# Out-projection of a hybrid decoder trunk: six DeltaNet heads by seven products of 2x2 blocks, in the middle of the stage

## The chip, the core and the metric

The kernel runs on one core of one Trainium2 chip. The metric is the device time of one execution in microseconds. Before the change it is 1019.95 us, the median of three runs (1019.5 to 1020.04).

A core has five engines with queues of their own, which run in parallel and wait for each other through semaphores: TensorE (PE, matrix products; PEld is its weight load), VectorE (DVE), ScalarE (ACT), GpSimd (POOL) and SyncE (SP, which here only issues DMAs). Each queue is worked off in order. SBUF is the working memory of 128 partitions, PSUM the memory in eight banks into which TensorE writes.

## What is computed

One decoder layer over 512 tokens and 16 meta tokens, with a model width of 2048. A normalised input goes through one input projection; three mixers run on disjoint heads: gated DeltaNet (6 heads of 128), GLA linear attention (5 heads) and forgetting attention (5 heads, "fox"). Their gated outputs, 6 x 128 + 5 x 128 + 5 x 128 = 2048 columns, go through one output projection, the input is added, and a final RMSNorm follows. Cut to the end, which is what the change touches:

```python
    o_dn = gated_head_norm(o_dn, dz, dn_norm_w.astype(f32))
...
    o_gla = gated_head_norm(o_gla, gz, gla_norm_w.astype(f32))
...
    o_fox = o_fox.reshape(fz.shape) * jax.nn.silu(fz)

    o = jnp.concatenate([o_dn, o_gla, o_fox], axis=-1)[:, PAD:].astype(x.dtype)
    return x + o @ w_out
...
    return rms_norm(h, final_norm_w)[:, N_META:]
```

All inputs and the output are float32.

## The kernel before

**Precision.** The two big projections run as products of split operands: each float32 operand is split into hi (a rounded copy in fp32r, made by ScalarE) and lo (the rest, a subtraction on VectorE). A product is three matmuls: hi by hi, hi by lo, lo by hi (the helper `mms`, line 992; the splits of weights are lines 149 and 150, with a high priority for the planner).

**The planner.** The code is written with a framework that gives each instruction a priority by its place in the program, plays the program on a timeline with assumed durations, and writes down for each engine a fixed order. An instruction of a later part can stand ahead where an earlier one isn't ready on that timeline. Buffers are taken from pools in the same way: a tile waits until one of its pool's buffers is free. So the matmuls of the next projection fill TensorE while a head's attention, a chain of small steps, goes on.

**Pools that matter here.** `wp`: raw, hi and lo buffers of 128x1024 for weights, two of each. `hp`: 32 buffers of 128x528, which hold the split input until the end of the input projection and then the split heads (`part`). `zp`: 11 buffers of 128x512 with the gated outputs of the DeltaNet and GLA heads (`zs`), later the accumulators `acc`. `six`: eight buffers of 128 x 1584, used by the mixers (a fox head takes four: q and k, the gate logits, the hi and the lo part of the probabilities) and by the last five accumulators. `psb` and `psm`: four PSUM banks each.

**Fox heads** (`fox_head`, lines 861 to 940). For each of five heads the projections fk, fv, fq, fz run (`inproj`, line 198; eight of its 128x1024 weight loads per head); then four blocks of 128 queries: scores (lines 903, 904), a softmax on VectorE and ScalarE (907 to 917), transposes (920), hi and lo (923, 924), and one product with the values (936 to 939) which is multiplied into the gate (940). For heads 2 to 4 the gate lies in the tile of the logits.

**The output projection** (from line 976). The 16 heads are the 16 blocks of the sum (six `dz`, five `gz`, five `fz`). `split_o` splits a head into `oh` and `ol` (984, 985). `acc[tb, cc]` is one of 4 x 4 blocks of the output (128 tokens x 512 columns); it is loaded with x by a DMA of ScalarE's queue (1036). For each of the four column blocks `cc`, `run` loads the weights of two heads (128 x 1024: two heads of 512 columns; DMA on SP's queue, line 141) and issues 2 x 4 x 3 matmuls into four banks. `add` (1009) adds a bank to `acc`, `square` (1016) sums its squares on ScalarE, `weigh` (1019) multiplies by the weight of the final norm on POOL. Column block 0 takes 14 heads first and the last two after column block 1. In the last column block the last six heads are done token block by token block from weights split ahead (`load_last`), and each token block is normalised and stored while the next one runs (1077 to 1088). In all, 16 heads x 4 x 4 x 3 = 768 matmuls, six of them (the end of the last token block) in two halves.

Of the kernel before, what the change touches and what calls it, by code (L numbers as in the profile page):

```python
# [8 lines left out]
F32 = mybir.dt.float32  # L9
F32R = mybir.dt.float32r  # L10
# [20 lines left out]
LOW = -87.0  # L31

DN_HEADS, GLA_HEADS, FOX_HEADS = 6, 5, 5
R0 = 32
R1 = R0 + 17

# [38 lines left out]


@with_exitstack
def tile_hybrid_trunk(ctx, tc, xT, xtok, mtok, w_gate, w_in, w_out, consts, lmask, fin_w, out, dbg=None):
# [17 lines left out]
    def t15(name, shape=(P, H, P), dt=F32):  # L96
        return wk.tile(list(shape), dt, tag="t15", bufs=6, name=name)
# [301 lines left out]
    def conv_silu(key, blk, dst, meta=True):  # L399

        t0 = 0 if meta else NM
        pb = row(f"pb{blk}")
        if meta:
            G.memset(pb[:, 0:3], 0.0)
        evac(inproj(key, first=0 if meta else NM - 4), pb, off=3)
        c = row(f"cv{blk}")[:, t0:T]
        V.tensor_scalar_mul(c, pb[:, t0:T], cwc[:, blk, 0:1])
        for w in range(1, 4):
            V.scalar_tensor_tensor(out=c, in0=pb[:, t0 + w : w + T], scalar=cwc[:, blk, w : w + 1], in1=c,  # L409
                                   op0=ALU.mult, op1=ALU.add)  # L410
        silu(dst[:, t0:], c, f"c{blk}")

    def bsl(b):
        return slice(NM + b * P, NM + (b + 1) * P)
# [446 lines left out]
    def fox_head(h):  # L861
# [78 lines left out]
        V.tensor_tensor(out=z, in0=po[:, :512], in1=z, op=ALU.mult)  # L940


    PM = (308, 319)
    for g in range(2):
        for h in range(max(NF, H * g), H * g + H):
# [25 lines left out]
    for mm, n in later:  # L971
# [2 lines left out]
            mybir.DependencyClass.NoSync, mybir.DependencyReason.DATA), reason="behind")  # L974


    heads = [("dz", h) for h in range(DN_HEADS)] + [("gz", h) for h in range(GLA_HEADS)] \
        + [("fz", h) for h in range(FOX_HEADS)]
    oparts = []

    def split_o(i):
        z = zs[heads[i]]
        hi, lo = part(f"oh{i}"), part(f"ol{i}")
        A.copy(hi, z)
        V.tensor_tensor(out=lo, in0=z, in1=hi.bitcast(F32), op=ALU.subtract)
        oparts.append((hi, lo))

    def mms(p_, hi, lo, i, tb, first, last, **kw):
        s = slice(tb * P, (tb + 1) * P)
        oh, ol = oparts[i]  # L990
        for n, (o_, w_) in enumerate(((oh, hi), (oh, lo), (ol, hi))):
            PE.matmul(p_, o_[:, s], w_, start=(first and n == 0), stop=(last and n == 2), **kw)  # L992

    FIRST, LAST = 14, 10
    halves = lambda w: [[t[:, j * 512 : (j + 1) * 512] for t in w] for j in range(2)]
    acc, wl = {}, {}

    def load_last(kp):
        raw = wp.tile([P, 1024], F32, tag="raw", name=f"rawl{kp}")
        nc.sync.dma_start(out=raw, in_=w_out[3, kp])  # L1000
        wl[kp] = []
        for j in range(2):
            hi, lo = part(f"wlh{kp}{j}"), part(f"wll{kp}{j}")
            split(raw[:, j * 512 : (j + 1) * 512], hi, lo)
            wl[kp].append((hi, lo))

    def add(tb, cc, p_, c=slice(0, 512)):
        a = acc[tb, cc][:, c]
# [12 lines left out]
    def run(pa, cc, kp, first, last):  # L1021
        w = halves(load_half(w_out[cc, kp], f"o{cc}_{kp}"))
        for j in range(2):
            for tb in range(4):
                mms(pa[tb], *w[j], 2 * kp + j, tb, first and j == 0, last and j == 1)

    for i in range(FIRST):
        split_o(i)
    fw = []
    for cc in range(4):  # L1030
        for tb in range(4):
            if 4 * cc + tb < 11:
                acc[tb, cc] = zp.tile([P, S], F32, tag="zs", name=f"acc{cc}{tb}")
            else:
                acc[tb, cc] = six.tile([P, S], F32, tag="six", name=f"acc{cc}{tb}")
            nc.scalar.dma_start(out=acc[tb, cc], in_=xtok[tb * P : (tb + 1) * P, cc * 512 : (cc + 1) * 512])
        pa = [psb.tile([P, 512], F32, tag="b", name=f"pa{cc}{tb}") for tb in range(4)]
        n = (FIRST // 2, KT // 2, KT // 2, LAST // 2)[cc]
        for kp in range(n):
            run(pa, cc, kp, kp == 0, kp == n - 1)  # L1040
            if cc == 3 and kp >= 2:
                load_last(kp + 3)
        if cc == 3:
            break
        for tb in range(4):
            add(tb, cc, pa[tb])
            if cc > 0:
                square(tb, cc)
        if cc == 0:
            for i in range(FIRST, KT):  # L1050
                split_o(i)
        if cc == 1:
            pb = [psm.tile([P, 512], F32, tag="m", name=f"pb{tb}") for tb in range(4)]
            run(pb, 0, FIRST // 2, True, True)
            for tb in range(4):
                add(tb, 0, pb[tb])
                square(tb, 0)
    for c in range(4):
        f = part(f"fw{c}").bitcast(F32)
        nc.scalar.dma_start(out=f, in_=fin_w[c * 512 : (c + 1) * 512].partition_broadcast(P))  # L1060
        fw.append(f)
    for cc in range(3):
        for tb in range(4):
            weigh(tb, cc)
    add(3, 3, pa[3], slice(256, 512))
    for tb in range(4):
        cuts = 2 if tb == 3 else 1
        for n in range(cuts):
            c = slice(512 // cuts * n, 512 // cuts * (n + 1))
            p_ = psm.tile([P, 512], F32, tag="m", name="pz") if n else pa[tb]  # L1070
            for i in range(LAST, KT):
                hi, lo = wl[i // 2][i % 2]
                mms(p_[:, c], hi[:, c], lo[:, c], i, tb, n == 1 and i == LAST, i == KT - 1, skip_group_check=True)
            add(tb, 3, p_, c)
            square(tb, 3, c, n)
        r = rr[:, tb : tb + 1]
        V.reduce_sum(r, ss[:, tb, : 3 + cuts], axis=mybir.AxisListType.X)
        A.activation(r, r, AF.Ln, scale=1.0 / D, bias=eps_c)
        A.activation(r, r, AF.Exp, scale=-0.5)
        for cc in (0, 1, 2, 3):  # L1080
            a = acc[tb, cc]
            if cc % 2 == 0:
                A.activation(a, a, AF.Copy, scale=r)
            elif cc == 3:
                V.scalar_tensor_tensor(out=a, in0=a, scalar=r, in1=fw[cc], op0=ALU.mult, op1=ALU.mult)
            else:
                V.tensor_scalar_mul(a, a, r)
            nc.sync.dma_start(out=out[tb * P : (tb + 1) * P, cc * 512 : (cc + 1) * 512], in_=a)


def _layout(x, meta_tokens, norm_w, w_in, conv_w, a_log, dt_bias, dn_norm_w, w_gk2, b_gk,
# [11 lines left out]
    wo = w_out[0].reshape(KT // 2, 2, P, 4, 512)  # L1103
    z6, z5 = np.zeros(6, f), np.zeros(5, f)
    one6, one5 = np.ones(6, f), np.ones(5, f)
    misc = np.zeros((P, 8), f)
# [21 lines left out]
        "w_out": c(wo.transpose(3, 0, 2, 1, 4).reshape(4, KT // 2, P, 1024)),  # L1128
        "consts": c(consts), "lmask": c(lm), "fin_w": c(np.asarray(final_norm_w)),
    }  # L1130

# [14 lines left out]
```

## Time and profile before

| | |
|---|---|
| median of the runs | 1019.95 us |
| the profiled execution | 1018.81 us |
| its span, first to last instruction | 1017.1 us |
| mean granted TensorE clock | 0.998 |
| first and last start of a matmul of the output projection | 825.7 and 1008.9 us |
| end of the last fox head's attention | 870 us |
| DMA traffic | 105 MB, 103 GB/s on average |

The profile is of one execution. "Busy" is the time in which an engine worked on instructions; matmuls are pipelined and overlap, so TensorE's busy time says that it was fed, not how fast it went. An arrow `out<-in` names the tile written and the tiles read; `L992` is line 992 of the kernel. "Idle before" is what an engine did not work just ahead of an instruction, with the instruction that ended the wait.

### The profile page before, as it was taken

To read this page: it belongs to the slowest core of one execution; us is meant where nothing else is said; L and a number is where in the kernel's file an instruction comes from. 1 tells how busy PE (TensorE), PEld (TensorE's weight loads), DVE (VectorE), ACT (ScalarE), POOL (GpSimd) and SP (SyncE) were. 2 spreads that over 40 slices of the span, in tenths; PEclk is the share of its full clock that TensorE was granted. 3 is DMA by queue.
4 is the path that set the end of the run, shared out by engine and by line. 5 is a ranking of instruction groups with operands and counts; after the bars stand their busy time and mean duration, and the time that the engine had idled before them with its cause. 6 is when DMAs were issued, how large, how long until landed. Compare 5 with 4: busy or idle time off the path is not lost.

```text
span 1017.1 us, 18766 instructions
## 1 busy us (share of the span) xinstructions
PE 1006.3 (99%) x7662; PEld 907.4 (89%) x7662; DVE 558.2 (55%) x1226; ACT 416.5 (41%) x916; POOL 135.5 (13%) x141
## 2 busy tenths in 40 slices
PE   9999999999999999999999999999999999999996
PEld 8899999899999888998999979898989888888885
DVE  6376867856566984343838373544444474323333
ACT  7653533443456333344544434333333362223224
POOL 0021411211112221100110021010101000000014
PEclk9999999999999999999999999999999999999999
DMA  9623133233221333222122222322223263232244
GB/s 356 221 68 131 65 99 105 83 100 104 91 79 64 98 104 100 71 79 70 63 65 69 67 92 63 94 92 70 92 82 92 85 204 128 83 104 90 96 145 166
DMA packets 42410, 105.03 MB, mean 103 GB/s; under 512 B 10733, under 2 KB 13981, under 8 KB 42324
## 3 DMA queue, kind: packets, MB, share of 16 engines
q1 hardware_dynamic: 28064, 92.23, 27.3%
q10 hardware_dynamic: 14260, 11.61, 4.1%
q8 instruction: 60, 0.98, 0.4%
q14 instruction: 26, 0.21, 0.1%
HBM read 98.64 MB, written 5.05 MB: 102 GB/s over the span
## 4 chain that ended last, share of the span: by engine, by line
PE 92%; DVE 3%; ACT 2%; DMA 1%; POOL 1%; issue 1%; ACTq 1%; DVEq 0%; POOLq 0%
PE pp L198 57%; PE pa L992 16%; PE pp L252 4%; PE pss L773 1%; POOL stgz L325 1%; PE pgate L352 1%; PE pfo L936 1%; PE pfa L903 1%; DVE ot L507 1%; DVE wlo L150 1%; PE pg L474 1%; PE pa L615 1%; PE py L639 1%; DMA sc<-ab 1%; PE pb L992 1%
## 5 line engine op out<-in xcount | busy, mean ns | idle before, releaser
L198 PE MATMUL pp<-xl,whi 128*128 128x264 f32 (+2 forms) x1456 | 378.6, 310 | 0.0
L198 PE MATMUL pp<-xh,whi 128*128 128x264 f32 (+2 forms) x1456 | 376.1, 310 | 0.1
L198 PE MATMUL pp<-xh,wlo 128*128 128x264 f32 (+2 forms) x1456 | 375.2, 309 | 0.4 <-DVE wlo L150 0.4
L198 PEld LDWEIGHTS pp<-xl,whi 128*128 128x128 f32 x1456 | 244.4, 189 | 13.6 <-issue 0.2
L198 PEld LDWEIGHTS pp<-xh,wlo 128*128 128x128 f32 x1456 | 243.6, 188 | 14.2 <-DVE wlo L150 0.9
L198 PEld LDWEIGHTS pp<-xh,whi 128*128 128x128 f32 x1456 | 243.0, 188 | 14.5 <-issue 0.8
L149 ACT CAST whi<-raw 128x1024 fp32r<-128x1024 f32 x110 | 115.4, 1049 | 201.5 <-PE pp L198 159.8
L150 DVE TENSOR_TENSOR wlo<-raw,whi 128x1024 fp32r<-128x1024 f32 x110 | 134.6, 1224 | 108.5 <-ACT whi L149 98.2
L992 PE MATMUL pa<-whio,ol 128*128 128x512 f32 x224 | 88.1, 393 | 0.0
L992 PE MATMUL pa<-wloo,oh 128*128 128x512 f32 x224 | 88.0, 393 | 0.0
L150 DVE TENSOR_TENSOR wloo<-rawo,whio 128x1024 fp32r<-128x1024 f32 x29 | 35.9, 1236 | 81.2 <-ACT whio L149 81.2
L992 PE MATMUL pa<-whio,oh 128*128 128x512 f32 x224 | 78.0, 396 | 0.0
L149 ACT CAST whio<-rawo 128x1024 fp32r<-128x1024 f32 x29 | 30.4, 1050 | 83.7 <-PE pa L992 65.1
L992 PEld LDWEIGHTS pa<-whio,ol 128*128 128x128 f32 x224 | 42.1, 188 | 9.8
L992 PEld LDWEIGHTS pa<-wloo,oh 128*128 128x128 f32 x224 | 42.1, 188 | 9.4
L992 PEld LDWEIGHTS pa<-whio,oh 128*128 128x128 f32 x224 | 41.9, 188 | 9.2
L325 POOL TENSOR_SCALAR stc<-cv 128x528 f32<-128x528 f32 (+1 forms) x18 | 28.2, 1564 | 138.3 <-DVE cv L409 115.3
L409 DVE SCALAR_TENSOR_TENSOR cv<-pb,cpk,cv 128x528 f32<-128x528 f32 (+1 forms) x54 | 40.8, 755 | 0.7
L1019 POOL TENSOR_TENSOR acc<-acc,fw 128x512 f32<-128x512 f32 x12 | 15.7, 1349 | 159.1 <-DMA fw<-in_fin_w 159.1
L316 DVE TENSOR_TENSOR pb<-pp,rstd 128x264 f32<-128x264 f32 (+1 forms) x36 | 13.7, 422 | 23.3 <-PE pp L198 23.3
L507 DVE TENSOR_TENSOR ot<-ab 51x30 f32<-51x30 f32 (+14 forms) x60 | 21.2, 354 | 3.6 <-DMA ab<-scmeta 2.1
L325 POOL TENSOR_SCALAR stfz<-zfz 128x512 f32<-128x512 f32 x5 | 9.8, 1965 | 99.0 <-ACT whi L149 49.0
(391 smaller groups left out, 1285.4 us busy)
## 6 DMA issues: line engine op xcount, KB each, us to landing
raw<-in_w_in SPq DMA_DIRECT2D x110, 512.0 KB, 3.3
rawo<-in_w_out SPq DMA_DIRECT2D x29, 512.0 KB, 3.3
xt<-in_xtok SPq DMA_DIRECT2D x8, 512.0 KB, 9.8
acc<-in_xtok ACTq DMA_DIRECT2D x16, 256.0 KB, 5.1
out<-acc SPq DMA_DIRECT2D x16, 256.0 KB, 3.0
xs<-in_xT SPq DMA_DIRECT2D x7, 528.0 KB, 6.7
gb<-gd ACTq DMA_DIRECT2D x2, 792.0 KB, 6.1
eg<-gd ACTq DMA_DIRECT2D x8, 192.0 KB, 3.4
```

What stands on the lines that cost most here:

```text
L149: A.copy(hi, raw)
L150: V.tensor_tensor(out=lo, in0=raw, in1=hi.bitcast(F32), op=ALU.subtract)
L198: mm = PE.matmul(p_[:, :nt], wt[:, j * m : (j + 1) * m], xx[k][:, t0 : t0 + nt], start=(k == 0 and wt is hi and xx is xh), stop=(k == KT - ...
L252: mm = PE.matmul(ps[:, :S], wt[:, j * P : (j + 1) * P], xx[k][:, NM:T], start=(k == 0 and wt is hi and xx is xh), stop=(k == KT - 1 and wt ...
L316: V.tensor_tensor(out=o, in0=p_[rows], in1=rstd[rows, t0 : t0 + n], op=ALU.mult)
L325: G.tensor_scalar_max(t, src, LOW)
L352: PE.matmul(pgate[a][:, :HT], wg[k // 8][:, k % 8, :], xx[k][:, a * HT : (a + 1) * HT], start=(k == 0 and xx is xh), stop=(k == KT - 1 and ...
L409: V.scalar_tensor_tensor(out=c, in0=pb[:, t0 + w : w + T], scalar=cwc[:, blk, w : w + 1], in1=c, op0=ALU.mult, op1=ALU.add)
L474: PE.matmul(pg[:r, j * r : (j + 1) * r], kT[:, j, ts], kT[:, j, ts], start=True, stop=True)
L507: V.tensor_tensor(out=t3, in0=a3[:, j + 1 :, j : j + 1].to_broadcast([NN * 4 + H, m, j]), in1=a3[:, j : j + 1, 0:j].to_broadcast([NN * 4 + ...
L992: PE.matmul(p_, o_[:, s], w_, start=(first and n == 0), stop=(last and n == 2), **kw)
L1019: G.tensor_tensor(out=acc[tb, cc], in0=acc[tb, cc], in1=fw[cc], op=ALU.mult)
```

## The change

The rows of the output projection's weights that belong to the DeltaNet heads (768) are taken out of the plain loops and multiplied by a scheme of seven products instead of eight, on blocks of 2 x 2. The left operand is cut by tokens (first and second 256) and by heads (even and odd of a pair, three pairs): a11, a12 (first tokens, even and odd head), a21, a22. The right one is cut by heads and by columns (first and second 1024). With sums of blocks on both sides,

- on the left: s1 = a21 + a22, s2 = s1 - a11, s3 = a11 - a21, s4 = a12 - s2 (on VectorE, in place, `sums`, `differences`), each split into hi and lo by `operand`;
- on the right (x, y, z in `weight_sums`): three differences and one more are computed from w_dn and kept in DRAM (`tw`);
- seven products (`product`): 3 pairs x 4 banks x 3 matmuls each, four of them going on in banks that hold an earlier product; after each, `take` adds four banks to four `acc` blocks.

The weight sums don't depend on the activations. They are made in `fox_head` of heads 0 to 3 in six pieces (pair and column half), each in one tile of `six`: four loads of 256 KB, four subtractions of 128 x 512, four stores of 256 KB, the DMAs on SP's queue.

The order of the stage becomes: the first eight of the ten other heads for column blocks 0 and 1, with the making of the operands between the loads; the seven products; the last two heads for column blocks 0 and 1; ten heads for column block 2; four heads for column block 3; and the end as before. Every third load of a product has its raw, hi and lo buffers in `six` (`load_s`). The first five `acc` blocks lie in `zp`, the others three to a tile of `six`. The loads of the final norm's weight stand before column blocks 0 and 1's last heads.

```diff
+    tw = drp.tile([SH // 2, 4, P, 1024], F32, name="tw")
+
+    def weight_sums(j, half):
+        c = slice(512 * half, 512 * half + 512)
+        w = six.tile([P, 3, 512], F32, tag="six", name=f"ws{j}{half}")
+        x, y, z = (w[:, i] for i in range(3))
+        get = lambda o, i, J: nc.sync.dma_start(out=o, in_=w_dn[J, 2 * j + i][:, c])
+        put = lambda n, t: nc.sync.dma_start(out=tw[j, n][:, c], in_=t)
+        sub = lambda o, a, b: V.tensor_tensor(out=o, in0=a, in1=b, op=ALU.subtract)
+        get(x, 0, 1)
+        get(y, 0, 0)
+        get(z, 1, 1)
+        sub(y, x, y)
+        sub(x, z, x)
+        sub(z, z, y)
+        put(0, y)
+        put(2, x)
+        put(1, z)
+        get(x, 1, 0)
+        sub(x, x, z)
+        put(3, x)
...
+        if h in SUMS:
+            for j, half in SUMS[h]:
+                weight_sums(j, half)
...
+    SUMS = {0: [(0, 0)], 1: [(0, 1), (1, 0)], 2: [(1, 1), (2, 0)], 3: [(2, 1)]}
...
+    EARLY, LAST = NP - 2, NP - 6
...
+    def operand(n):
+        for j in pairs:
+            t, r = part(f"{n}_{j}"), raw[j][n]
+            A.copy(t[:, t0], r)
+            sub(t[:, t1], r, t[:, t0].bitcast(F32))
+            ops[n, j] = [t[:, t0], t[:, t1]]
...
+    rest = lambda a, b: [split_o(i) for i in range(a, b)]
+    steps = [lambda: rest(4, EARLY), lambda: operand("a11"), lambda: (operand("a12"), sums()),
+             lambda: (differences(), operand("s2")), lambda: operand("s1"), lambda: rest(EARLY, NP)]
+    rest(0, 4)
+    for cc in range(2):
+        for tb in range(4):
+            begin(tb, cc)
+        pa = banks(psb, f"pa{cc}")
+        for kp in range(EARLY // 2):
+            run(pa, cc, kp, kp == 0, kp == EARLY // 2 - 1)
+            if steps:
+                steps.pop(0)()
...
+    def load_s(src, name):
+        nw[0] += 1
+        if nw[0] % 3:
+            return load_half(src, name)
+        raw = six.tile([P, 1024], F32, tag="six", name=f"raw{name}")
+        nc.sync.dma_start(out=raw, in_=src)
+        hi, lo = (six.tile([P, 1024], F32R, tag="six", name=f"w{i}{name}") for i in ("hi", "lo"))
+        split(raw, hi, lo)
+        return hi, lo
+
+    def product(p_, n, weights, first, last):
+        for j in pairs:
+            w = halves(load_s(weights(j), f"{n}{j}"))
+            for k in range(4):
+                tb, c = k // 2, k % 2
+                mms(p_[k], ops[n, j], w[c], slice(tb * P, (tb + 1) * P), first and j == 0, last and j == pairs[-1])
...
+    product(pa, "a11", lambda j: w_dn[0, 2 * j], True, True)
+    take(pa, 0, 0)
+    product(pb, "a12", lambda j: w_dn[0, 2 * j + 1], True, True)
+    take(pb, 0, 0)
+    product(pa, "s2", lambda j: tw[j, 1], False, True)
+    take(pa, 0, 1)
+    pb = banks(psm, "ps")
+    product(pb, "s1", lambda j: tw[j, 0], True, True)
+    take(pb, 1, 1)
+    product(pa, "s3", lambda j: tw[j, 2], False, True)
+    take(pa, 1, 1)
+    product(pb, "s4", lambda j: w_dn[1, 2 * j + 1], False, True)
+    take(pb, 0, 1)
+    product(pa, "a22", lambda j: tw[j, 3], False, True)
+    take(pa, 1, 0)
```

More of the change, by code (lines that the diff above doesn't have):

```diff
@@ L33 @@
 DN_HEADS, GLA_HEADS, FOX_HEADS = 6, 5, 5
+SH = 6
 R0 = 32
@@ L981, in split_o @@
+    oparts = {}
     def split_o(i):
-        z = zs[heads[i]]
+        z = zs[plain[i]]
         hi, lo = part(f"oh{i}"), part(f"ol{i}")
         A.copy(hi, z)
[L985 to L992, printed above, removed]
@@ L994, in tile_hybrid_trunk @@
-    FIRST, LAST = 14, 10
+        sub(lo, z, hi.bitcast(F32))
+        oparts[i] = hi, lo
+    t0, t1 = slice(0, 256), slice(256, 512)
+    pairs = range(SH // 2)
+    raw, ops = {}, {}
+    for j in pairs:
+        a, b = (zs[heads[2 * j + i]] for i in range(2))
+        raw[j] = dict(a11=a[:, t0], a12=b[:, t0], a21=a[:, t1], a22=b[:, t1])
+    def operand(n):
[4 more added lines that the diff above has]
+            ops[n, j] = [t[:, t0], t[:, t1]]
@@ new lines, in tile_hybrid_trunk, with begin, mms @@
+    acc, wl = {}, {}
+    free = []
+    def begin(tb, cc):
+        if len(acc) < 11 - SH:
+            acc[tb, cc] = zp.tile([P, S], F32, tag="zs", name=f"acc{cc}{tb}")
+        else:
+            if not free:
+                t = six.tile([P, 3, 512], F32, tag="six", name=f"accs{len(acc)}")
+                free.extend(t[:, i] for i in range(3))
+            acc[tb, cc] = free.pop(0)
+        nc.scalar.dma_start(out=acc[tb, cc], in_=xtok[tb * P : (tb + 1) * P, cc * 512 : (cc + 1) * 512])
+    def mms(p_, o, w, s, first, last):
+        for n, (o_, w_) in enumerate(((o[0], w[0]), (o[0], w[1]), (o[1], w[0]))):
+            PE.matmul(p_, o_[:, s], w_, start=(first and n == 0), stop=(last and n == 2), skip_group_check=True)
@@ L1024, in run, with banks @@
             for tb in range(4):
-                mms(pa[tb], *w[j], 2 * kp + j, tb, first and j == 0, last and j == 1)
-    for i in range(FIRST):
-        split_o(i)
+                mms(pa[tb], oparts[2 * kp + j], w[j], slice(tb * P, (tb + 1) * P), first and j == 0, last and j == 1)
+    def banks(where, name):
+        if where is psb:
+            return [psb.tile([P, 512], F32, tag="b", name=f"{name}{k}") for k in range(4)]
+        return [psm.tile([P, 512], F32, tag="m", name=f"{name}{k}") for k in range(4)]
@@ new lines, in sums, with differences @@
+    def sums():
+        for j in pairs:
+            r = raw[j]
+            if j % 2 == 0:
+                s1 = row(f"os{j}")
+            r["s1"] = s1[:, t1 if j % 2 else t0]
+            V.tensor_tensor(out=r["s1"], in0=r["a21"], in1=r["a22"], op=ALU.add)
+            sub(r["a21"], r["a11"], r["a21"])
+            r["s3"] = r["a21"]
+    def differences():
+        for j in pairs:
+            r = raw[j]
+            sub(r["a11"], r["s1"], r["a11"])
+            r["s2"] = r["a11"]
+    rest = lambda a, b: [split_o(i) for i in range(a, b)]
@@ new lines, in tile_hybrid_trunk @@
+    steps = [lambda: rest(4, EARLY), lambda: operand("a11"), lambda: (operand("a12"), sums()),
[9 more added lines that the diff above has]
+                steps.pop(0)()
+        for tb in range(4):
+            add(tb, cc, pa[tb])
@@ new lines, in tile_hybrid_trunk @@
+    for f in steps:
+        f()
+    for j in pairs:
+        r = raw[j]
+        sub(r["a12"], r["a12"], r["s2"])
+        r["s4"] = r["a12"]
+    operand("s3")
+    operand("s4")
+    operand("a22")
+    nw = [0]
+    def load_s(src, name):
[7 more added lines that the diff above has]
+        return hi, lo
@@ new lines, in product, with take @@
+    def product(p_, n, weights, first, last):
+        for j in pairs:
+            w = halves(load_s(weights(j), f"{n}{j}"))
+            for k in range(4):
+                tb, c = k // 2, k % 2
+                mms(p_[k], ops[n, j], w[c], slice(tb * P, (tb + 1) * P), first and j == 0, last and j == pairs[-1])
+    def take(p_, h, J):
+        for k in range(4):
+            add(2 * h + k // 2, 2 * J + k % 2, p_[k])
+    for cc in range(2, 4):
+        for tb in range(4):
+            begin(tb, cc)
@@ L1029, in tile_hybrid_trunk @@
+    take(pb, 0, 1)
+    product(pa, "a22", lambda j: tw[j, 3], False, True)
+    take(pa, 1, 0)
     fw = []
+    for c in range(4):
+        f = part(f"fw{c}").bitcast(F32)
+        nc.scalar.dma_start(out=f, in_=fin_w[c * 512 : (c + 1) * 512].partition_broadcast(P))
+        fw.append(f)
     for cc in range(4):
[L1031 to L1042, printed above, removed]
+        pa = banks(psb if cc % 2 else psm, f"pt{cc}")
+        kps = ((NP // 2 - 1,), (NP // 2 - 1,), range(NP // 2), range(LAST // 2))[cc]
+        for kp in kps:
+            run(pa, cc, kp, kp == kps[0], kp == kps[-1])
+            if cc == 2 and kp >= NP // 2 - 3:
+                load_last(kp)
@@ L1046, in tile_hybrid_trunk @@
             add(tb, cc, pa[tb])
[L1047 to L1061, printed above, removed]
+            square(tb, cc)
     for cc in range(3):
```

29 lines of the change are left out of this document (16 added, 13 removed).

## The prediction, made before the result was known

> **What bounds the kernel now.** I read the page's first part, then the waits of TensorE, then the windows and the chain of the output projection.
>
> ```profile
> span 1017.1 us, 18766 instructions
> ...
> PE 1006.3 (99%) x7662; PEld 907.4 (89%) x7662; DVE 558.2 (55%) x1226; ACT 416.5 (41%) x916; POOL 135.5 (13%) x141
> ```
>
> ```profile
> PE warm L247 <- POOL ones L110: 1.2, 1, 1.2
> PE psn L645 <- ACT y L641: 0.6, 1, 0.6
> PE pss L773 <- issue: 0.6, 1, 0.6
> PE pp L198 <- DVE wlo L150: 0.4, 1, 0.4
> ```
>
> The second fence is the whole list of what TensorE waited for: 2.8 us in four places, none of them at a line of the output projection (L992). So TensorE is the bound from the first matmul to the last, and the other engines matter only where they make it wait. The windows (columns: length, then busy us of each engine, granted clock, DMA share, GB/s) show the attention of the last heads, the overlap of attention and projection, and two stretches of projection alone:
>
> ```profile
> 740.00:800.00 60.00, 60.00 (x396) 54.66 (x395) 26.83 (x70) 19.22 (x36) 4.06 (x4) 1.00 0.27 85
> ...
> 826.00:870.00 44.00, 44.00 (x204) 35.96 (x204) 23.79 (x58) 16.60 (x31) 2.46 (x2) 1.00 0.43 142
> 870.00:920.00 50.00, 50.00 (x218) 40.71 (x217) 16.14 (x18) 12.73 (x20) 0.00 (x0) 1.00 0.30 95
> 920.00:975.00 55.00, 55.00 (x240) 44.74 (x239) 17.27 (x18) 15.75 (x26) 0.00 (x0) 1.00 0.28 90
> ```
>
> One caution first: the profile models a matmul's end, so its "busy 0.39 us" is longer than its share of the time. What one matmul costs is the pitch, and the chain of waits gives it:
>
> ```profile
> 870.38 44.34 PE pa L992 x192
> 914.71 5.54 PE pb L992 x24
> 920.25 55.43 PE pa L992 x240
> ```
>
> 44.34 / 192, 5.54 / 24 and 55.43 / 240 are all 0.231 us, at a granted clock of 1.00. VectorE is busy a third of this stretch (16.14 of 50), ScalarE a quarter.
>
> **The change part by part.**
>
> *Matmuls.* Before, the six DeltaNet heads take 6 heads x 4 token blocks x 4 column blocks x 3 terms = 288 matmuls of 512 columns. After, each of seven products takes 3 pairs of heads x 4 banks x 3 terms = 36, so 252. The ten other heads keep 480. Removed: 36 x 0.231 = **8.3 us**, all on the bounding engine. TensorE's waits reach nowhere near this stage, so there is no idle time there to win beside it: 8.3 us is the most that can go. The shape, the weight load per matmul and the type stay, so the pitch should.
>
> The Trainium skill, page "TensorE: Matmul & The Clock Gate", section "Back-to-back issue gap", puts a warm matmul of N columns at N / 2.4 + 2.5 ns, 216 ns for 512; the trace differs, with 231. By the page, the estimate of the gain is 36 x 0.216 = 7.8 us instead of 8.3; I keep the measured pitch.
>
> *Weights of the products.* A plain load of 128x1024 weights (two heads, 512 columns) feeds 24 matmuls, 5.54 us of TensorE. A load for a product (one pair, 1024 columns) feeds 12, 2.77 us. There are 21 of these, and 20 plain ones, against 32 before. What a load and the additions cost, as groups of instructions between 826 and 1008 us (busy us, mean ns of one, then idle time before them):
>
> ```profile
> L150 DVE TENSOR_TENSOR wloo<-rawo,whio 128x1024 fp32r<-128x1024 f32 x28 | 34.6, 1237 | 80.6 <-ACT whio L149 80.6
> L1009 DVE TENSOR_TENSOR acc<-acc,pa 128x512 f32<-128x512 f32 x15 | 10.3, 686 | 6.3 <-PE pa L992 6.2
> L985 DVE TENSOR_TENSOR ol<-fc,oh 128x512 fp32r<-128x512 f32 x3 | 2.0, 682 | 0.7 <-ACT oh L984 0.7
> ...
> L149 ACT CAST whio<-rawo 128x1024 fp32r<-128x1024 f32 x28 | 29.4, 1050 | 83.2 <-PE pa L992 65.1 <-issue 10.0 <-DMA rawo<-in_w_out 7.4
> L984 ACT CAST oh<-fc 128x512 fp32r<-128x512 f32 x3 | 1.8, 618 | 1.9 <-DVE fc L940 1.9
> ```
>
> A subtraction of 256 columns, the size of the new operands, has this row from an earlier stage (min/median/max ns):
>
> ```profile
> L759 DVE TENSOR_TENSOR kq<-gqk,gdd x14: 409/410/419, 548.1 to 612.9; 128x256 f32<-128x256 f32 x7, 64x256 f32<-64x256 f32 x7
> ```
>
> VectorE in the product stage: 21 weight subtractions x 1.237 = 26.0, 28 additions of banks into acc x 0.686 = 19.2, and the late operands (s3, s4, a22: nine splits and three differences x 0.41) 4.9: 50.1 us in 252 x 0.231 = 58.2 us of TensorE, 86%. In the first four products, where the late operands fall, it is 14.8 + 11.0 + 4.9 = 30.7 of 33.3 us, 92%. That is the tightest place of the change. ScalarE has 21 x 1.05 + 9 x at most 0.62 = 27.6 us there, under half.
>
> Does the pipeline of weights still keep ahead? One load of today:
>
> ```profile
> 931.17 1.08 PE L992 MATMUL pa<-whio,oh 128*128 128x512 f32 x4
> 931.37 1.05 ACT L149 CAST whio<-rawo 128x1024 fp32r<-128x1024 f32 x1 [4.45 <-PE pa L992]
> ...
> 932.45 1.23 DVE L150 TENSOR_TENSOR wloo<-rawo,whio 128x1024 fp32r<-128x1024 f32 x1 [4.27 <-ACT whio L149]
> ```
>
> At 931.17 TensorE turns to the next load and frees a buffer; the split into it ends at 933.68, 2.5 us later. With two buffers that is needed 5.54 us after the release (3.0 us spare), and for a product 2.77 us after it (0.3 us spare, which one 0.69 us addition ahead of it in VectorE's queue would use up). But every third load goes to buffers in `six`, so a buffer set comes round after three loads: the split has 2 x 2.77 = 5.54 us again. The raw buffer's round is the load's landing, the split and perhaps an addition, in 3 x 2.77 = 8.31 us:
>
> ```profile
> rawo<-in_w_out SPq DMA_DIRECT2D x29, 512.0 KB, 3.3
> acc<-in_xtok ACTq DMA_DIRECT2D x16, 256.0 KB, 5.1
> out<-acc SPq DMA_DIRECT2D x16, 256.0 KB, 3.0
> ...
> raw2q<-in_w_in SPq DMA_DIRECT2D x4, 256.0 KB, 7.0
> ```
>
> (DMA issues: size of one, median us to landing.) The view of the tile rawo adds its extremes:
>
> ```profile
> DMA to landing us min/median/max: 3.1/3.3/4.6
> ```
>
> With the slowest, 4.6 + 2.5 + 0.7 = 7.8 us, still inside 8.31. So in the sum the product stage has no steady loss. Misses are possible, since VectorE's queue is in order and 86 to 92% full. Bounds: nothing, since no row shows TensorE waiting at L992; at most one addition exposed per product, 7 x 0.686 = 4.8 us. No gain can hide here (TensorE never waits in this stage now). I take **1.0 us given back**, nearer the rows, which show none.
>
> *The products' additions* read a bank which the next-but-one product continues: a whole product, 36 x 0.231 = 8.3 us, lies between, against four additions, 2.7 us. Hidden; without that cover 2.7 us each.
>
> *Operands before the products* (sums, differences, a11, a12, s2, s1: 9 + 12 operations of 0.41 us, 8.6 us on VectorE) fall beside the first two column blocks, 192 matmuls, 44 us, while the last attention head also runs: 23.79 + 8.6 = 32.4 of 44 us busy, 74%. The 3.0 us spare of the plain loads hides them. The six 0.68 us splits of the DeltaNet heads, which stood just ahead of this window, go.
>
> *Order of the stage.* The last attention head ends at 870; its gate product was needed near the end of the second column block, and is now needed after 192 plain and 252 product matmuls, so later. Its delay costs nothing.
>
> *Weight sums.* Six tiles, in heads 0 to 3: each four loads and four stores of 256 KB on SP's queue and four subtractions of 128x512 on VectorE, 24 x 0.68 = 16.3 us over some 190 us, where VectorE is busy 26.83 of 60. ScalarE gets nothing, POOL nothing. The traffic is 48 x 0.26 = 12.6 MB, some 65 GB/s on top of 85. On SP the splits' loads stand behind them:
>
> ```profile
> SPq L141 <- DVE wlo L150: 586.3, 87, 15.7
> ```
>
> SP issues a weight load when the subtraction frees its buffer, 6.7 us apart on average (586.3 / 87). A freed buffer is wanted again about 11 us later (two loads of 5.5), less 3.3 for landing and 2.5 for the split: some 5 us of SP standing still are hidden. A store waits for its subtraction, the reload of x for its store (3.0 us by out<-acc): with 5.1 for a load each, some 14 us of chain per tile, which the order of the queue must thread between loads. I take nothing for it. Upper end: one whole chain in the way, 14 - 5 = 9 us.
>
> The tiles come from `six`. A head holds four of its eight; the next head's first two are written meanwhile, and the gates of heads 2 to 4 stay in one each. So two are spare up to head 2, one or two at head 3. If none is, the head's hi and lo wait, and the chain of attention gets longer:
>
> ```profile
> 634.69 0.17 DVE L907 CUSTOM_DVE_ANT_0 fp<-pfa,fc 128x16 f32<-128x16 f32 x1 [2.90 <-issue]
> ...
> 673.24 0.69 DVE L940 TENSOR_TENSOR fz<-pfo,fz 128x512 f32<-128x512 f32 x1 [0.26 <-PE pfo L939]
> ...
> 676.98 0.17 DVE L907 CUSTOM_DVE_ANT_0 fp<-pfa,fc 128x16 f32<-128x16 f32 x1
> ```
>
> Head 0's takes 38.6 us and head 1's starts 3.7 us after it, all beside the projections of head 1, so a few us more there change the order on TensorE and not its work. Nothing.
>
> *End.* The last six heads of the last column block are the same 72 matmuls, and what follows them (to 1017.1) is the same. The weighing on POOL can start earlier; it isn't last now. Nothing.
>
> **Sum.** Span 1017.1 - 8.3 + 1.0 = 1009.8. The profiled execution took 1018.81 in all, 1.7 over its span; the median of the runs is 1.1 above that. So 1019.95 - 7.3 = **1012.6 us**.
>
> **Rivals.**
>
> *VectorE in the product stage becomes the bound in places.* For: 92% in the first four products, additions and splits in one queue. Against: the planner puts splits ahead. Price 4.8 us: 1019.95 - 8.3 + 4.8 = 1016.5.
>
> *SP's queue in the attention.* One chain of a sums tile stops the weight loads: 9 us against 8.3, 1020.6, no change. Against: only three of the 1017 us show TensorE short of anything, and the loads are few.
>
> *Landing time, and slower.* The products draw 512 KB per 2.77 us, 189 GB/s, twice the 95 of the row 870 to 920. If landing grows past 8.31 - 3.2 = 5.1 us, each load costs TensorE a third of the excess of the round. At the 7.0 us of the first loads (raw2q), a round takes 10.2, or 3.4 a load: 21 x 0.63 = 13.2 us, so 1019.95 - 8.3 + 13.2 = 1024.9. It decides from 5.1 us and outweighs the gain from 6.3 us. Against it: 4.6 is rawo's slowest, in a stretch with 142 GB/s.
>
> *That fewer matmuls are not run* is excluded: the loops give 732 against 768.
>
> **How the numbers follow.** Forecast 0.69 (own range 1011.0 to 1014.5), VectorE 0.16, SP 0.08, landing 0.07. The range takes in the first two and leaves 0.15 to the others: 1011.0 (8.3 gone, nothing given back, less the spread of the runs) to 1018.0. What a measurement here can tell from no change is about 0.2%, 2.0 us: faster 0.85, same 0.08, slower 0.07.
>
> **What would show it.** Right: 732 matmuls of the stage at 0.231 us, still no wait of TensorE at the matmuls of the projection over 1 us in all, the weight splits in the products waiting for TensorE and not the reverse, raw loads landing under 5 us. Wrong: waits of TensorE for wlo or whi of the products (VectorE, if additions stand just ahead; landing, if the splits wait for DMA), for wlo in the attention (SP), or a pitch other than 0.231.

## The result and the profile after

The changed kernel takes 1011.99 us (median of five runs, 1010.78 to 1012.03), the kernel before 1019.95 on the same chip. The ratio is 0.9923, with a 95% interval of 0.9912 to 0.9934. On a second chip the ratio was 0.9934 [0.9921, 0.9946].

The page of the changed kernel, its first lines:

```profile
span 1010.3 us, 18941 instructions
...
PE 997.9 (99%) x7626; PEld 900.7 (89%) x7626; DVE 609.3 (60%) x1318; ACT 428.7 (42%) x940; POOL 137.3 (14%) x141
```

There are 36 matmuls fewer on TensorE, 51 us more work on VectorE, and the share of TensorE is 99% as before: the bound has not changed. All that TensorE waited for (line, releaser, us in total, times, longest):

```profile
PE warm L248 <- POOL ones L111: 1.2, 1, 1.2
PE pp L253 <- ACT whi1q L150: 0.7, 1, 0.7
PE pp L199 <- DVE fqk L317: 0.7, 1, 0.7
PE psn L670 <- ACT y L666: 0.6, 1, 0.6
PE pg L842 <- ACT gkm L833: 0.5, 1, 0.5
PE pss L798 <- issue: 0.5, 1, 0.5
```

None of the six is at L1050, where the matmuls of the output projection are now. The chain of the changed kernel through the seven products and into the plain loads behind them (start, us, engine, tile, line, matmuls):

```profile
877.45 8.27 PE pq L1050 x36
885.72 8.31 PE pr L1050 x36
894.02 8.36 PE pq L1050 x36
902.38 8.29 PE ps L1050 x36
910.67 8.29 PE pq L1050 x36
918.96 8.31 PE ps L1050 x36
927.27 8.38 PE pq L1050 x36
935.65 44.35 PE pt L1050 x192
```

Each product takes 8.27 to 8.38 us, 0.230 to 0.233 a matmul, the pitch of the plain loads on both sides. The whole stage is dense.

Where the 6.8 us between the two spans (1017.1 and 1010.3) come from is best read from the starts of the same matmuls in both traces. The in-projection's 4368 matmuls are the same in all kernels of this case, in nearly the same order, so their starts are a clock for everything ahead of the output projection:

| after minus before, us | |
|---|---|
| first in-projection matmul of L198/L199 | +1.21 |
| number 3000 (560 us) | +0.56 |
| the last (825 us) | +1.51 |
| first to last matmul of the output projection: 183.13 to 174.73 | -8.40 |
| last matmul to end: 8.23 to 8.34 | +0.11 |

The first row lies in the first 62 us, before anything that the change touches. In the other kernels below, with the same program there, it lies between 0.05 and 1.35, so it is not the change's. The stage itself won 8.40 us, and 0.95 were lost between number 3000 and the last matmul, where the weight sums are made.

### The profile page after: what moved, and what is told of

The parts are those of the page before. It is cut to its first block, busy times and chain, and to the rows that moved or that the text cites. A ratio compares the mean times of both kernels' runs of the same rounds, so it can differ in the third digit from the quotient of the medians.

```text
span 1010.3 us, 18941 instructions
## 1 busy us (share of the span) xinstructions
PE 997.9 (99%) x7626; PEld 900.7 (89%) x7626; DVE 609.3 (60%) x1318; ACT 428.7 (42%) x940; POOL 137.3 (14%) x141
## 4 chain that ended last, share of the span: by engine, by line
PE 98%; DMA 1%; ACT 0%; issue 0%; DVE 0%; SPq 0%; ACTq 0%; DVEq 0%
PE pp L199 63%; PE pt L1050 6%; PE pa L1050 4%; PE pp L253 4%; PE pq L1050 3%; PE ps L1050 2%; PE pss L798 1%; PE pr L1050 1%; PE pgate L353 1%; PE pfo L964 1%; PE pfa L931 1%; DMA raw1q<-in_w_in 1%; PE pg L499 1%; PE pa L640 1%; PE py L664 1%; PE pfx L948 1%
## 5 line engine op out<-in xcount | busy, mean ns | idle before, releaser
L199 PE MATMUL pp<-xl,whi 128*128 128x264 f32 (+2 forms) x1456 | 378.3, 310 | 0.0
L199 PE MATMUL pp<-xh,whi 128*128 128x264 f32 (+2 forms) x1456 | 375.9, 310 | 0.8 <-DVE fqk L317 0.7
L199 PE MATMUL pp<-xh,wlo 128*128 128x264 f32 (+2 forms) x1456 | 375.4, 309 | 0.0
L199 PEld LDWEIGHTS pp<-xh,whi 128*128 128x128 f32 x1456 | 243.1, 188 | 15.1 <-issue 1.5
L199 PEld LDWEIGHTS pp<-xl,whi 128*128 128x128 f32 x1456 | 244.4, 189 | 13.6 <-issue 0.2
L199 PEld LDWEIGHTS pp<-xh,wlo 128*128 128x128 f32 x1456 | 243.7, 189 | 13.7 <-DVE wlo L151 0.4
L151 DVE TENSOR_TENSOR wloo<-rawo,whio 128x1024 fp32r<-128x1024 f32 x17 | 22.7, 1337 | 20.2 <-ACT whio L150 20.2
L150 ACT CAST whio<-rawo 128x1024 fp32r<-128x1024 f32 x17 | 17.8, 1050 | 28.6 <-DMA rawo<-in_w_out 12.5
L1050 PE MATMUL pt<-whio,ol 128*128 128x512 f32 x72 | 28.3, 393 | 0.0
L1050 PE MATMUL pt<-wloo,oh 128*128 128x512 f32 x72 | 28.2, 392 | 0.0
L1050 PE MATMUL pa<-wloo,oh 128*128 128x512 f32 x64 | 25.4, 396 | 0.0
L940 ACT ACTIVATE fp<-fp,fsm 128x144 f32<-128x144 f32 (+3 forms) x20 | 11.5, 575 | 32.5 <-DVE fsm L939 32.5
L1050 PE MATMUL pa<-whio,ol 128*128 128x512 f32 x64 | 25.2, 393 | 0.0
L1050 PE MATMUL pt<-whio,oh 128*128 128x512 f32 x72 | 24.6, 395 | 0.0
L1050 PE MATMUL pa<-whio,oh 128*128 128x512 f32 x64 | 23.6, 399 | 0.0
```

The costliest lines, as they stand in the source:

```text
L150: A.copy(hi, raw)
L151: V.tensor_tensor(out=lo, in0=raw, in1=hi.bitcast(F32), op=ALU.subtract)
L199: mm = PE.matmul(p_[:, :nt], wt[:, j * m : (j + 1) * m], xx[k][:, t0 : t0 + nt], start=(k == 0 and wt is hi and xx is xh), stop=(k == KT - ...
L940: A.activation(pr[:, : m + P], pr[:, : m + P], AF.Exp, bias=sm[:, 2:3], accum_out=sm[:, 3:4])
```

## The experiments

Twelve runs were made, in four groups, each beside the kernel before on its chip. The table has the median, the ratio to the kernel before, and from each one's trace two lengths: what the in-projection fell behind the kernel before between its matmul 3000 and its last one, and the output projection from its first to its last matmul start.

| | us | ratio [95%] | lost in the attention | output projection |
|---|---|---|---|---|
| before | 1019.95 | 1 | 0 | 183.13 |
| after | 1011.99 | 0.9923 [0.9912, 0.9934] | 0.95 | 174.73 |
| e1 sums only | 1020.52 | 1.0011 [1.0002, 1.0020] | 1.48 | 183.16 |
| e2 no sums | 1010.97 | 0.9920 [0.9906, 0.9933] | 0.03 | 174.66 |
| e3 two sets | 1018.78 | 0.9993 [0.9984, 1.0002] | 0.93 | 182.12 |
| e4 eighth product | 1022.88 | 1.0036 [1.0022, 1.0049] | 1.21 | 184.89 |
| e5 after again | 1013.0 | 0.9934 [0.9921, 0.9946] | 1.50 | 174.73 |
| e6 double additions | 1013.25 | 0.9938 [0.9920, 0.9956] | 0.99 | 176.23 |
| e7 four pairs | 1015.21 | 0.9955 [0.9943, 0.9968] | 0.97 | 177.17 |
| e8 five pairs | 1026.29 | 1.0063 [1.0050, 1.0075] | 1.04 | 188.90 |
| e9 sums moved | 1012.7 | 0.9942 [0.9929, 0.9956] | 1.01 | 174.82 |
| e10 four pairs, wide | 1010.69 | 0.9920 [0.9907, 0.9934] | 0.94 | 173.20 |
| e11 sums from head 1 | 1011.17 | 0.9914 [0.9898, 0.9931] | 0.15 | 174.88 |
| e12 wide, sums from head 1 | 1010.96 | 0.9910 [0.9891, 0.9928] | 2.68 | 173.20 |

The medians of one kernel differ by about 1 us from chip to chip (e5 and after are one program), so differences under 1 us are read from the two lengths and not from the medians. In the two traces of that one program the output projection took 174.73 us both times, while 0.95 and 1.50 us were lost in the attention: the length of the stage repeats closely, the loss only to about half a microsecond.

**The sums alone, and the products alone.** e1 adds `weight_sums` to the kernel before:

```diff
+        if h in SUMS:
+            for j, half in SUMS[h]:
+                weight_sums(j, half)
```

> The kernel before with the weight sums added in fox heads 0 to 3 and never read; the out-projection is the old one. Theory A (TensorE is the bound everywhere and the sums lie beside it): the time of the kernel before, 1020.0 us, within 0.7. Theory B (the 1.5 us by which the stage begins later in the changed kernel's trace, 827.3 against 825.7, is the price of the sums): 1021.5. Theory C (SP's queue stands at a store and weight loads come late): 1025 or more, with waits of TensorE for wlo between 580 and 800.

e2 takes them out of the changed kernel:

```diff
-        if h in SUMS:
-            for j, half in SUMS[h]:
-                weight_sums(j, half)
...
-    product(pa, "s2", lambda j: tw[j, 1], False, True)
+    product(pa, "s2", lambda j: w_dn[0, 2 * j], False, True)
```

> The changed kernel without the weight sums; the products that read sums read plain blocks of the same size instead, so the output leaves the sums out. Theory A: 1012.0 us, like the changed kernel, within 0.7. Theory B: 1010.5, and the first matmul of the out-projection 1.5 us earlier than with the sums.

e1 lost 1.48 us in the attention and nothing in the stage, e2 lost 0.03 there and won 8.47 in the stage. So the two parts of the change are separate, and the loss comes with the sums: 1 to 1.5 us, near theory B's size (by the medians e1 is 1.2 us over the kernel before of its chip). Theory B's 1.5 contained the start-up, which the first table takes apart. e2's first output matmul was only 0.4 us earlier than the changed kernel's, since at matmul 3000 it was already 1.09 us late, the changed kernel 0.56. Theory C is out: between 560 and 826 us TensorE never waited for wlo in the changed kernel. Of the six waits above, only two lie there: 0.7 us at L199, for fqk, and 0.5 us at L842, for gkm. In e2 neither is there, nor any other between these times. The stores did make SP stand, but briefly (SP's own waits in the changed kernel: us in total, times, longest; L423 is the store, L422 the load):

```profile
SPq L423 <- DVE ws L424: 9.5, 14, 1.7
SPq L422 <- DMA tw<-ws: 8.4, 5, 2.2
SPq L423 <- DVE fsm L937: 3.7, 2, 2.7
```

The longest stop is 2.7 us, under the 5 that the prediction counted as hidden.

**Where the 1 us comes from.** One of the two waits, in order of time in the changed kernel: VectorE clears a PSUM bank of head 1's fk projection late, and the next projection has to wait for it. Ahead of the clearing in VectorE's queue stands a softmax step of head 0 (L935), before which VectorE was idle for 0.99 us, waiting for scores from TensorE.

```profile
641.61 0.31 DVE L935 CUSTOM_DVE_ANT_0 fp<-pfa,fc 128x144 f32<-128x144 f32 x1 [0.99 <-PE pfa L931]
...
642.05 0.76 DVE L317 TENSOR_TENSOR fqk<-pp,rstd 128x264 f32<-128x264 f32 x2
...
642.62 0.47 PE L199 MATMUL pp<-xh,whi 128*128 128x512 f32 x1 [0.69 <-DVE fqk L317]
```

Nothing of the sums runs on VectorE just ahead of it; what differs is the order of the instructions from about 630 us on. In the changed kernel the four transposes of head 0's values (L895) are interleaved with four of a GLA head (L881):

```profile
630.08 0.28 PE L881 MATMUL pgt<-ident,gqk 128*128 128x128 f32 x1
...
630.20 0.27 PE L895 MATMUL pvf<-ident,vf 128*128 128x128 f32 x1
...
630.30 0.27 PE L881 MATMUL pgt<-ident,gqk 128*128 128x128 f32 x1
```

In the kernel before and in e2 the four of the values run together. Two experiments move the sums. e9 takes them out of head 1:

```diff
-    SUMS = {0: [(0, 0)], 1: [(0, 1), (1, 0)], 2: [(1, 1), (2, 0)], 3: [(2, 1)]}
+    SUMS = {0: [(0, 0), (0, 1)], 2: [(1, 0), (1, 1)], 3: [(2, 0), (2, 1)]}
```

> The changed kernel with the six pieces of sums in heads 0, 2 and 3, two each, and none in head 1. Theory A (the 1 us is one wait of TensorE for the evacuation of a projection at about 642 us, where the planner's order on VectorE put a softmax step of head 0 ahead of it because the sums shifted the order there; it is not the work of the sums): the pace of the in-projection falls back by a different amount, 0 to 0.3 us if no such place arises, 1011.2 where the changed kernel has 1012.0. Theory B (24 subtractions and 48 DMAs cost 1 us wherever they stand): 0.9 to 1.5 us lost again between the 3000th and the last matmul of the in-projection, in a different place.

The same wait of 0.69 stood at the same place, 641.7 us, and 1.01 us was lost: neither theory as it was written, since the place did not move. e11 takes them out of head 0:

```diff
-    SUMS = {0: [(0, 0)], 1: [(0, 1), (1, 0)], 2: [(1, 1), (2, 0)], 3: [(2, 1)]}
+    SUMS = {1: [(0, 0), (0, 1)], 2: [(1, 0), (1, 1)], 3: [(2, 0), (2, 1)]}
```

> The changed kernel with no sums in head 0; heads 1, 2 and 3 make two pieces each. Moving the pieces of head 1 left the wait for the evacuation at 642 us where it was; what the kernels with that wait have in common are sums in head 0, and in their traces the transposes just before 631 us come in another order. Theory A (a change of order by the sums of head 0, not their work): the wait is gone, the in-projection loses 0 to 0.3 us between its 3000th and its last matmul, 0.7 us less than the changed kernel in all. Theory B (the work of the sums costs about 1 us wherever it stands): 0.7 to 1.5 us lost there again.

Now both waits were gone and 0.15 us was lost, with the same 24 subtractions and 48 DMAs. The transposes run together again, as without sums. In e11:

```profile
629.11 0.27 PE L881 MATMUL pgt<-ident,gqk 128*128 128x128 f32 x1
...
629.22 0.60 PE L895 MATMUL pvf<-ident,vf 128*128 128x128 f32 x4
```

So the price is not that of the work. In all ten kernels of the table with sums in head 0, which run beside the last GLA heads, the transposes are interleaved, and all ten lost 0.93 to 1.50 us; in the four without (before, e2, e11 and e12) they run together. The order came with sums in head 0 and so did the loss; that it is the order just before 631 us which makes the loss is argued, not shown. The median's interval overlaps that of the changed kernel, so as a gain in time e11 is not shown either.

**What keeps the products fed.** e3 gives all their loads the two buffer sets of `wp`:

```diff
-        if nw[0] % 3:
+        if True:
             return load_half(src, name)
```

> The changed kernel with all weight loads of the products in the two buffers of wp, none in six. Theory A as the prediction has it (2.5 us from release to split, needed after 2.77, an addition of 0.69 may stand ahead): TensorE waits in the products, between 2 and 8 us in all, 1014 to 1020. Rival (the order that the planner writes absorbs it, the third set is not needed): 1012.0 and no wait of TensorE in the products.

The stage took 7.4 us longer (182.12 against 174.73) and nearly all of the gain was gone. The chain that ended last in e3, from 884 to 925 us, by share:

```profile
by line: DMA raws<-tw 40.4%; DVE wlos L151 20.4%; ACT whis L150 10.3%; DVE accs L1064 9.1%; DVE acc L1064 6.6%; issue 5.8%; DVE wloa L151 2.9%; ACT whia L150 2.6%; PE pq L1050 1.8%; DVE s L1010 1.1%; DVE a L1010 0.8%; ACTq L150 0.2%
```

and one round of it:

```profile
890.16 3.65 DMA raws<-tw
...
893.88 1.06 ACT whis L150
...
894.97 1.23 DVE wlos L151
...
896.71 0.68 DVE acc L1064
897.39 0.59 DVE accs L1064
897.99 1.14 DVE wlos L151
...
899.15 3.51 DMA raws<-tw
```

TensorE has nearly left the chain. A load lands, is split, two additions stand in VectorE's queue, the split of the other buffer's load follows, and then that buffer's next load starts. Other loads went out in between, at 892.16 and 896.22. From 890.16 to 928.29 us the loads start 3.18 us apart on average, where TensorE needs one every 2.77; a buffer comes round in 5.7 to 7.8 us instead of 5.54. Landing, hi and lo alone are 3.65 + 1.06 + 1.23 = 5.94 us, without any addition ahead of them. The waits are so many small ones that the list of TensorE's waits shows only 2.5 us of them; in the starts of the matmuls, 36 come late from 886 us on, by 7.2 us in all. The third set in `six` is worth 7.4 us, and without it the change is within 0.2% of no change.

**Is VectorE near its bound?** e6 does each addition of the products twice:

```diff
             add(2 * h + k // 2, 2 * J + k % 2, p_[k])
+            add(2 * h + k // 2, 2 * J + k % 2, p_[k])
```

> The changed kernel with each of the 28 additions of the products done twice, so the output counts the products twice; VectorE gets 28 x 0.68 = 19 us more in a stage of 58 us in which it is busy 45. Theory A (VectorE is near its bound in the products, splits and additions share one queue): 64 of 58 us, TensorE waits 5 us or more, 1017 to 1021. Rival (additions may lag by a product, since banks alternate, and the plain loads after them give the time back): 1012 to 1014.

The windows of the product stage, the changed kernel first, then e6 (length; busy us of PE, PEld, DVE, ACT, POOL; clock; DMA):

```profile
877.00:936.00 59.00, 59.00 (x257) 47.97 (x257) 44.25 (x58) 24.32 (x30) 0.00 (x0) 1.00 0.59 191
```

```profile
877.00:936.00 59.00, 58.25 (x251) 46.59 (x250) 54.24 (x77) 23.87 (x30) 0.00 (x0) 1.00 0.56 183
```

VectorE was 75% busy and then 92%, and the stage grew by 1.5 us only. The count of its instructions says why: 19 more of the 28 lie in this window and the others later. An addition may wait until its bank is wanted again, a product later, and TensorE waited 0.8 us in all for weight splits in the products. The rival held.

**Does the count of matmuls alone make the gain?** e4 runs the product of s4 twice:

```diff
     take(pa, 1, 0)
+    product(pb, "s4", lambda j: w_dn[1, 2 * j + 1], False, True)
+    take(pb, 0, 1)
```

> The changed kernel with an eighth product: the one of s4 is run twice and added twice, 36 matmuls, three loads and four additions more. Theory A (only the number of matmuls counts, 0.231 us each): 1012.0 + 8.3 = 1020.3, so the kernel before again. Rival (part of the gain comes from the new order and not from the count): the difference to the changed kernel is clearly off 8.3, under 6 or over 10.

The stage grew by 10.2 us (184.89 against 174.73), more than the 8.3 of its matmuls. It is 1.8 us longer than in the kernel before, so the expected equality failed, and the difference is over the 10 us that the rival names. The chain of e4 shows where they are:

```profile
936.53 8.31 PE ps L1050 x36
944.84 8.34 PE pt L1050 x36
...
953.21 0.69 DVE acc L1064
...
956.59 1.78 DVE wloo L151
...
958.42 3.75 PE pt L1050 x15
```

The eighth product itself costs 8.31: the matmuls have the price that was counted. The rest is lost in the plain loads behind it, where four matmuls start late, by 1.8 us in all. Four additions of a plain block stand ahead of a weight split in VectorE's queue, and wait for TensorE themselves. They start 8.4 us after the first plain matmul (944.84), in the changed kernel 3.5 us after it (935.65). The same four in e4, then in the changed kernel:

```profile
953.21 2.77 DVE L1064 TENSOR_TENSOR acc<-acc,pt 128x512 f32<-128x512 f32 x4 [2.79 <-PE pt L1050]
```

```profile
939.14 2.77 DVE L1064 TENSOR_TENSOR acc<-acc,pt 128x512 f32<-128x512 f32 x4 [1.55 <-PE pt L1050]
```

In e4 the split behind them (1.78 us on the chain) comes late; in the changed kernel it doesn't. So the rival's number was reached through a loss of e4's own, and not because part of the gain comes from the order: the changed kernel's stage is dense, and its 8.40 us are the 8.3 of the count. Why the planner's order came out so in e4 is not shown.

**How far does it go?** Four pairs (eight heads) and five pairs (ten), with the kernel's own constant and more pieces of sums:

```diff
-SH = 6
+SH = 8
...
-    SUMS = {0: [(0, 0)], 1: [(0, 1), (1, 0)], 2: [(1, 1), (2, 0)], 3: [(2, 1)]}
+    SUMS = {h: [(h, 0), (h, 1)] for h in range(4)}
```

> Eight heads in four pairs (six DeltaNet, two GLA) by seven products, eight pieces of sums. Theory A: 12 matmuls fewer than the changed kernel, 2.8 us, less 0.3 to 0.5 for two more pieces of sums: 1009.6 where the changed kernel has 1012.0. Rival (the cover of the first column blocks, 144 matmuls or 33 us instead of 44, gets too short for the operands and the last attention head): no gain, 1012 or more, with waits of TensorE before or in the first products.

> Ten heads in five pairs (six DeltaNet, four GLA), ten pieces of sums. Theory A: 24 matmuls fewer than the changed kernel, 5.5 us, less 0.7 for four more pieces of sums: 1007.2. Rival (cover of 96 matmuls, 22 us, for the operands of 20 head halves and for a last attention head that takes 44 us): TensorE waits before or in the first products, 1010 or more.

Both rivals held. The stage with four pairs took 177.17 us, where 12 matmuls fewer should have made it 172.0; with five it took 188.90. The windows of e7 show VectorE full while the operands are made (13.31 of 14 us):

```profile
854.00:868.00 14.00, 12.95 (x57) 9.68 (x56) 13.31 (x38) 6.70 (x15) 0.00 (x0) 1.00 0.39 132
```

against 32.01 of 50 us in the changed kernel:

```profile
827.00:877.00 50.00, 50.00 (x231) 40.87 (x230) 32.01 (x79) 19.35 (x37) 3.13 (x2) 1.00 0.47 160
```

The last attention head's steps, the operands and the splits share its queue there, and with 144 and 96 matmuls ahead there is not enough for TensorE to do meanwhile. In e8 even the attention waits:

```profile
PE pfx L948 <- DVE fp L945: 6.3, 1, 6.3
PE pq L1050 <- ACT whia L150: 3.0, 1, 3.0
```

e10 gives four pairs more cover, three column blocks of six heads instead of two:

```diff
-    for cc in range(2):
+    for cc in range(3):
         for tb in range(4):
             begin(tb, cc)
...
-        kps = ((NP // 2 - 1,), (NP // 2 - 1,), range(NP // 2), range(LAST // 2))[cc]
+        kps = ((NP // 2 - 1,), (NP // 2 - 1,), (NP // 2 - 1,), range(LAST // 2))[cc]
...
-            if cc == 2 and kp >= NP // 2 - 3:
-                load_last(kp)
+            if cc < 3:
+                load_last(NP // 2 - 3 + cc)
```

> Four pairs again (48 matmuls fewer than the kernel before instead of 36), but three column blocks of six heads ahead of the products: 216 matmuls or 50 us of cover where the first try with four pairs had 144 or 33 us and waited. Theory A (that try lost its gain to the short cover of the operands): the waits before the products go, 2.8 us less than the changed kernel and 0.4 for two more pieces of sums: 1009.5 where the changed kernel has 1012.0. Rival (the loss came from VectorE's work, the accumulators in six or the buffers of the products): 1012 or more, with the waits in the products.

The stage fell to 173.20 us, 4.0 under e7 with the same products: the cover was the cause of most of e7's loss of 5.2. Of the 2.8 us of 12 matmuls 1.5 came through; one wait remains in front of the products:

```profile
PE pa L1050 <- DVE accs L1064: 0.9, 1, 0.9
```

e12 puts its eight pieces of sums into heads 1 to 3:

```diff
-    SUMS = {h: [(h, 0), (h, 1)] for h in range(4)}
+    SUMS = {1: [(0, 0), (0, 1), (1, 0)], 2: [(1, 1), (2, 0), (2, 1)], 3: [(3, 0), (3, 1)]}
```

> Four pairs with three column blocks ahead of the products, as before, and the eight pieces of sums in heads 1 to 3 (three, three, two). Theory A: 0.7 us less than four pairs with three column blocks and sums in heads 0 to 3 (ratio to the kernel before 0.991). Theory B, or a shortage of six with three pieces a head: no better, with the loss in the in-projection.

The loss in the attention went up to 2.68 us, 2.4 of them between matmuls 3450 and 3600 of the in-projection (652 to 684 us). Its chain there runs through the sums themselves:

```profile
656.88 2.58 DMA ws<-in_w_dn
...
661.55 5.70 DMA ws<-in_w_dn
...
667.35 0.69 DVE ws L424
...
668.06 3.09 DMA tw<-ws
...
671.21 2.57 DMA ws<-in_w_dn
...
673.81 0.69 DVE ws L424
```

Load, subtraction, store, reload, subtraction, each behind the other, with VectorE's queue standing in between. So the three pieces in head 1 cost more here than the two of e11. The number alone does not do it: e8, with three pieces in heads 1 and 2, lost 1.04 us in the attention.

And the changed kernel once more:

> The changed kernel once more, beside the others of this group. Theory A': 36 matmuls of 0.231 us gone, about 1 us given back, and that in the attention (where the kernels with sums fall 1.0 to 1.5 us behind between the 3000th and the last matmul of the in-projection, and the one without sums none): 7.3 us under the kernel before of the same chip. Rival (the 1.2 us at the start of the changed kernel's profile belongs to the change): the first matmul of line 199 late by about 1.2 us again in the profile of this run.

It was 6.5 us under the kernel before of its chip by the medians where 7.3 was expected, with 1.50 us lost in the attention; its stage was again 174.73 and its first in-projection matmul only 0.39 late, not 1.21: the start-up is not the change's.

Of all these e10 and e12 have the lowest medians, 1010.7 and 1011.0, and the intervals of their ratios lie wholly under 1. Against the changed kernel the intervals of their ratios overlap (0.9920 [0.9907, 0.9934] and 0.9910 [0.9891, 0.9928] against 0.9923 and 0.9934), so a better version is likely and not shown.

## Why the prediction was right

Predicted 1012.6, measured 1011.99. The spans of the two profiled executions differ by 6.8 us, where 7.3 was predicted, the medians by 8.0; closer than that it can't be judged, since medians of one program move by 1 us from chip to chip. By its steps:

- **36 matmuls of 0.231 us, 8.3.** Right: the stage lost 8.40 us and the products run at 0.230 to 0.233 a matmul. e2, without sums, has 8.47. The Trainium skill (page "TensorE: Matmul & The Clock Gate", section "Back-to-back issue gap") gives 216 ns as the isolated gap of a warm matmul of 512 columns, and about 131 ns for a stream with a weight load for each matmul. The products have weight loads and ran at neither. The trace counts 750 starts, not 732: 18 matmuls at the end run in two halves, not six as the description of the kernel has it, and the same 18 before.
- **1.0 us given back.** The size was right and the place wrong, so that the sum came out by luck here. It was put down to VectorE's queue in the products, where TensorE did not wait at all: without this term the products alone would have given 1011.65. It was lost in the attention, 0.95 us (1.50 in e5), a part which the prediction took at nothing: a few us more in a head's chain would change the order on TensorE and not its work. The order did change, and with it came two waits of TensorE, 0.7 and 0.5 us.
- **VectorE 86 to 92% busy in the products.** Oversized: 44.25 of 59 us, 75%, and in the first four products, where 92% was expected, 24.68 of 34 us (877 to 911), 73%. Two things were missed. Instructions that follow each other overlap by some 0.06 us (the 58 instructions of this window add up to 48.1 us, the busy time is 44.25). And the additions don't have to keep up: e6 brought VectorE to 92% and it cost 1.5 us, not 4.8. So the condition of the rival that was given 0.16 was not met.
- **The third set of buffers carries the products.** Right and decisive (e3, 7.4 us). The prediction found the two-set case short if an addition stood ahead of the split. What closed first in e3 was the raw buffer's round, 5.7 to 7.8 us against 5.54, which is short already without an addition (5.94).
- **Landing.** The product loads landed in 3.6 us in the median:

```profile
DMA to landing us min/median/max: 3.4/3.6/6.2
```

  (the tile raws of the changed kernel; rawa has 3.2/3.6/5.0). The median is far under the 5.1 from which the slower rival was to decide. The slowest one is over it, and over the 5 us that was named as a sign of being right, but no product waited for it. The room was smaller than the prediction has it: between 877 and 936 us the weight splits waited 14.9 us for loads and 14.5 us for TensorE.
- **SP's queue.** Right for the changed kernel: the longest stop for a store or reload is 2.7 us. e12 shows a chain of loads and stores that does cost time, though it reaches TensorE through VectorE's queue and the attention, not through late weight loads.
- **Operands beside the first column blocks, hidden.** Right with 192 matmuls of cover; e7 and e8 show the price when it is 144 or 96.
- **The end.** Right: 8.34 us behind the last matmul's start against 8.23.

## What to carry to other kernels

In a kernel whose bounding engine is dense, what is taken off it comes out in full if three things hold: its operands are made beside enough other work, the buffers go round with a spare set at the faster pace, and the work that may lag (here the additions) does not stand ahead of the work that may not (the splits). Work put "beside" a dense stage can cost more in one place than in another (here 1 us or 0.15), so move it and measure before blaming its size. Waits of a few tenths add up without standing out in a list of waits; the length of a stage between two known instructions shows them.

## What the hardware showed

In e8 TensorE stood idle for long stretches between 852 and 878 us, and the granted clock (the number behind the busy times) fell after that:

```profile
852.00:860.00 8.00, 6.49 (x28) 4.50 (x27) 8.00 (x21) 2.29 (x4) 0.00 (x0) 1.00 0.52 166
860.00:870.00 10.00, 2.48 (x11) 1.51 (x9) 10.00 (x26) 5.92 (x15) 0.00 (x0) 0.78 0.46 158
870.00:878.00 8.00, 4.61 (x14) 3.70 (x14) 2.80 (x7) 3.36 (x9) 0.00 (x0) 0.50 0.50 164
878.00:885.00 7.00, 6.97 (x21) 5.57 (x22) 2.11 (x2) 1.35 (x2) 0.00 (x0) 0.66 0.24 75
```

It is 0.50 from 865.69 us, 4.3 us after the end of a matmul that was followed by a pause of 6 us, to 882.76 us, 4.7 us after TensorE took up the dense product again (878.03). The 4.61 us of work between 870 and 878 did not bring it back. The idle time is paid for a second time: the first eleven matmuls from 878.03 us on take 4.80 us, where 11 x 0.231 would be 2.54. The Trainium skill describes such a gate (page "TensorE: Matmul & The Clock Gate", Part 1): half the clock after an idle window of about 3.4 us, the full one after a busy window of the same length. This trace agrees in the halving, with 0.50; its delays, 4.3 and 4.7 us, are somewhat longer than one such window. In the kernel before and the changed one the clock is below 1.00 only behind the last matmul.
